# Query and key tiles in descending order in the attention and mLSTM tasks of a two-block transformer kernel

## The chip, the cores and the metric

The kernel runs on one core of one Trainium2 chip. The metric is device time in microseconds for one execution; lower is better.

## What is computed

Two transformer blocks follow one another on a sequence of 512 tokens with 1024 features, all in float32. The first has a mixer with two kinds of attention and a mixture of experts; the second has a mixer of native sparse attention and an mLSTM, a cross attention on a memory, and a feed-forward layer. The change touches only these parts (cut from the reference):

```python
# block 1, forget attention: 8 heads of 64; F is the running sum of log gates
s = jnp.einsum('bhqd,bhkd->bhqk', qb, k) * scale + Fq[..., :, None] - F[..., None, :]
p = jax.nn.softmax(jnp.where(pos[None, :] <= tq[:, None], s, -jnp.inf), axis=-1)
o = jnp.einsum('bhqk,bhkd->bhqd', p, v)
# block 1, differential attention: 4 heads, two maps of 64, values of 128
p1 = jax.nn.softmax(jnp.where(mask, s1, -jnp.inf), axis=-1)
p2 = jax.nn.softmax(jnp.where(mask, s2, -jnp.inf), axis=-1)
o = jnp.einsum('bhqk,bhkd->bhqd', p1 - lam * p2, v)
# block 2, sparse attention: 8 heads of 64 in 2 groups, three branches
return gc[..., 0:1] * o_c + gc[..., 1:2] * o_s + gc[..., 2:3] * o_w
# block 2, mLSTM: 4 heads, queries and keys of 64, values of 128
s = jnp.einsum('bthd,bshd->bhts', qc, kc) * w
num = jnp.einsum('bhts,bshv->bhtv', s, vc) + ...
```

All maps are causal (or causal by chunks), so query tile i of 128 rows needs key tiles 0 to i only.

## The kernel before

Everything is tiled by 128. A sequence is four query tiles (NT = 4). The program is written for a framework that inserts the semaphores and lets a compiler put the instructions of each engine in an order by a model of their times; the order of the program is their priority, not their final order. Projections are float32 products in three matmuls (`mm3`, lines 149 to 154: high by high, high by low, low by high).

**Tasks.** Attention is cut into tasks, each with a map of four query tiles: 8 Fox tasks (class `Fox`, line 444, one per head), 4 Diff tasks (class `Diff`, line 468), 16 NSA tasks (class `Nsa`, line 1420, two per head: b = 0 for the selected and b = 1 for the window branch), and 4 mLSTM cells (class `Cell`, line 1754). A task has these methods:

- `a(i)`: the scores of query tile i against key tiles 0 to i, 128*(i+1) wide, on TensorE into one of two "sc" banks (lines 440, 1468); `softmax_rows` (line 229) adds the bias and takes the row minimum on VectorE (line 237), then the exponential on ScalarE (line 239), into a tile "sx". Fox scales the row at once (lines 454, 455). Diff combines two maps into one row (lines 479 to 483). NSA scales rows in pairs after every second step (lines 1474 to 1483: factors L1476 and L1477, rows by VectorE at L1483, but row 2 by ScalarE at L1481).
- The transposes of the task: `transposer32` (line 260) makes key tile j of the transposed map in one of two "tr" banks: 4-j transposes, from rows j to 3 (line 269), then one copy (line 270) by ScalarE for even j and by VectorE for odd j.
- `finish`: the product of the transposed map with the values. Fox and NSA do it for two heads at a time, 16 matmuls of 64 columns (`apply_pair`, line 275, L280), so in every second Fox task and in the tasks of odd NSA heads; Diff (L495) and Cell (L1795) do it for each task. All begin with key tile 0.

**Order.** A task's rows are computed while the task before is transposed. Step i of four, in ascending order, is `cur.a(i)`, some fill, `trs(i)` of the task before, some fill; after the fourth step comes `prev.finish`. For Fox and Diff this loop is in `mixer1` (lines 526 to 546), for NSA and the cells in `run_tasks` (line 1219).

**Fill.** Projections wait in a queue in units of one k tile (three matmuls, `queue_proj`, line 117); `fill(n)` emits n of them. Fox emits one unit after every `a` and every `trs`; Diff one or two, in the last Diff task nearly none; NSA 1.25 a step after `a` and none after `trs`; the cells one after each.

**Beside the tasks.** In NSA, the short convolution of the mLSTM inputs runs in single steps (`conv`, line 1401: ScalarE L1410, GpSimd L1411, L1414, L1415); two steps are taken per task, after `a(0)` and `a(1)`, from the second head on. The lower halves of split weights go to GpSimd there (`share(0, 1)`, line 1534; L219), to VectorE elsewhere. In b = 1 tasks the next head's compressed branch is begun after `a(1)` (`compressed`, line 1431) and transposed after `a(3)` (`compressed_T`, line 1455, L1459).

**Buffers.** Rows are tiles "sx" of 128 x 512: 9 in mixer1 (SX) and 8 in the second block (SN). Diff's second map, the values before their transposition (`vt`, line 1392), the convolution temporary (`ct`, line 1409) and the cells' output (`yt`, line 1808) take tiles of the same rotation.

Of the kernel before, what the change touches and what calls it, by code (L numbers as in the profile page):

```python
# [30 lines left out]
SX = 9  # L31
SN = 8

# [61 lines left out]
class Builder:  # L95
# [132 lines left out]

    def softmax_rows(self, ps_s, i, win, pool, bufs, rs=None):

        nc = self.nc
        n = P * (i + 1)
        s = pool.tile([P, S], F32, tag="sx", name="sx", bufs=bufs)
        mn = pool.tile([P, 1], F32, tag="mn", name="mn", bufs=8)
        if rs is None:
            rs = pool.tile([P, 1], F32, tag="rs", name="rs", bufs=16)
        nc.vector.tensor_tensor_reduce(out=s[:, :n], in0=ps_s[:, :n], in1=win[:, S - P - P * i:S], scale=1.0,  # L237
                                       scalar=3.0e38, op0=ALU.add, op1=ALU.min, accum_out=mn)
        nc.scalar.activation(s[:, :n], s[:, :n], AF.Exp, bias=mn, scale=-1.0, accum_out=rs)  # L239
        return s, rs  # L240
# [97 lines left out]
    def mixer1(self, x_dram, outer, before_gates, before_out):  # L338
        nc, tc, a = self.nc, self.tc, self.a
        w_in = a["w_in"][0]  # L340
        with ExitStack() as st:
# [26 lines left out]
            with ExitStack() as sa:  # L368
# [75 lines left out]
                class Fox:  # L444
                    def __init__(s, h, box):
                        s.h, s.r, s.box, s.rows = h, h % 2, box, []

# [3 lines left out]
                    def a(s, i):  # L451
# [3 lines left out]
                        nc.vector.tensor_scalar_mul(p[:, :P * (i + 1)], p[:, :P * (i + 1)], rs)  # L455
                        s.rows.append(p)

# [10 lines left out]
                class Diff:  # L468
                    def __init__(s, h, box):
                        s.h, s.box, s.rows = h, box, []  # L470

# [3 lines left out]
                    def a(s, i):  # L475
                        n = P * (i + 1)
                        p1, r1 = self.softmax_rows(scores(s.box, 0, i), i, win[:, 1 + s.h], wk, SX)
                        p2, r2 = self.softmax_rows(scores(s.box, 1, i), i, win[:, 1 + s.h], wk, SX)
                        nc.vector.reciprocal(r2, r2)
# [3 lines left out]
                        nc.vector.scalar_tensor_tensor(p1[:, :n], p2[:, :n], r2, p1[:, :n], op0=ALU.mult, op1=ALU.add)  # L483
                        s.rows.append(p1)

# [29 lines left out]
                for g in range(8):  # L515
# [10 lines left out]
                    for r in range(2 if g < 4 else 1):  # L526
                        cur = Fox(2 * g + r, boxes[g]) if g < 4 else Diff(g - 4, boxes[g])
                        cur.start()
                        if prev is not None:
                            trs = self.transposer32(prev.rows, wk, pst, 3)  # L530
                        for i in range(NT):
                            cur.a(i)
                            self.fill(per[2 * i])
                            if prev is not None:
                                trs(i)
                            self.fill(per[2 * i + 1])
                        if prev is not None:
# [4 lines left out]
                trs = self.transposer32(prev.rows, wk, pst, 3)  # L542
                for j in range(NT):
                    trs(j)
# [674 lines left out]
    def run_tasks(self, tasks, slots, more, wk, pst, before, bufs):  # L1219

        prev, self.credit = None, 0
        for n, cur in enumerate(tasks + [None]):
# [3 lines left out]
            trs = self.transposer32(prev.rows, wk, pst, bufs) if prev is not None else None  # L1226
            for i in range(NT):
                if cur is not None:
# [65 lines left out]
    def mixer2(self, hT, sl, right):  # L1294
# [8 lines left out]
        with ExitStack() as sa:  # L1303
# [84 lines left out]
            def queue_v(h):  # L1388
                w = self.cols(w_in, 1816 + h * P)

                def done(z):
                    vt = wk.tile([P, S], F32, tag="sx", name="vt", bufs=SN)
                    nc.scalar.copy(vt, z)
# [7 lines left out]
            def conv(m):  # L1401
# [5 lines left out]
                for d in (3, 2, 1):  # L1407
                    c = 4 * (3 - d) + m
                    ct = wk.tile([P, S], F32, tag="sx", name="ct", bufs=SN)
                    nc.scalar.activation(ct[:, d:], u[:, :S - d], AF.Copy, scale=cw[:, c:c + 1])  # L1410
# [9 lines left out]
            class Nsa:  # L1420


                def __init__(s, h, b, head):
                    s.h, s.b, s.g, s.head, s.rows = h, b, h // 4, head, []

# [37 lines left out]
                def a(s, i):  # L1463
# [6 lines left out]
                    p, _ = self.softmax_rows(z, i, s.head["tab"], wk, SN, s.rs[:, i:i + 1])  # L1470
                    s.rows.append(p)
                    if i in (0,1) and s.h:
                        next(convs, None)
                    if i % 2 == 1:
                        c = slice(i - 1, i + 1)
                        nc.vector.reciprocal(s.rs[:, c], s.rs[:, c])  # L1476
                        nc.vector.tensor_mul(s.rs[:, c], s.rs[:, c], gates[:, c, 3 * s.h + 1 + s.b])  # L1477
                        for m in (i - 1, i):
                            n = P * (m + 1)
# [4 lines left out]
                    if s.b == 1 and s.h < 7:  # L1484
                        if i == 1:
                            self.drain(boxes[(s.h + 1) // 2])
                            tasks[2 * s.h + 2].compressed()
                        elif i == 3:
                            tasks[2 * s.h + 2].compressed_T()
# [234 lines left out]
    def mlstm(self, w_in, hT, mq, mv, mg, sl, right, work):  # L1724
# [29 lines left out]
        class Cell:  # L1754
            def __init__(s, h):
                s.h, s.rows = h, []

# [5 lines left out]
            def a(s, i):  # L1763
# [11 lines left out]
                                               op0=ALU.mult, op1=ALU.add, accum_out=s.den[:, i:i + 1])  # L1775
                s.rows.append(w)
                if i == 1 and s.h > 1:
                    cells[s.h - 2].after()
# [23 lines left out]
            def after(s):  # L1802
                h, on = s.h, s.on
                pt = pst.tile([P, S], F32, tag="tr", name="tr")
                for i in range(NT):
                    nc.vector.tensor_scalar_mul(on[:, i], on[:, i], s.r[:, i:i + 1])
                    nc.tensor.transpose(pt[:, i * P:(i + 1) * P], on[:, i], self.ident)
                yt = wk.tile([P, S], F32, tag="sx", name="yt", bufs=SN)
                nc.vector.scalar_tensor_tensor(yt, sg[:, h], 1.0, pt, op0=ALU.add, op1=ALU.mult)
# [177 lines left out]
```

## Time and profile before

| | |
|---|---|
| time, median of 3 runs | 1842.98 us (1830.79 to 1845.54) |
| profiled execution | 1842.04 us |
| its span, first to last instruction | 1840.3 us |
| granted TensorE clock, mean of the span | 0.981 |
| TensorE (PE) matmul busy | 1754.1 us, 95% |
| VectorE (DVE) / ScalarE (ACT) / GpSimd (POOL) busy | 834.3 / 590.9 / 101.5 us |

Times come from one profiled execution. PE is the matmul part of TensorE, PEld its weight load. A name such as `sx<-sx,nrs` gives the tile written and the tiles read; L1483 is line 1483 of the kernel. The granted clock is a share of full speed: 1.00 is 2.4 GHz, 0.50 is 1.2 GHz.

### The profile page before, as it was taken

The page shows a single profiled execution, that of the slowest core. Times are in us where ns is not written, and L with a number is a line of the kernel's source. Part 1 is how long each engine was busy: PE and PEld are TensorE (multiplying, and loading weights), DVE is VectorE, ACT ScalarE, POOL GpSimd, SP SyncE. Part 2 cuts the span into 40 slices and gives each one's busy share as a digit, 9 for nine tenths or more (in the row PEclk, how much of TensorE's full clock was granted, in tenths as well). Part 3 has the DMA queues.
Part 4 walks back from the last instruction along what each step waited for, and adds up shares of the span by engine and source line. Part 5 has one row for each costly group of instructions (what it writes and reads, how often), then busy time and mean ns, then how long its engine had stood idle before and what let it go on. Part 6 is the DMA issues. An engine that isn't in the chain of part 4 may idle for free. (4 is left out here: it accounts for less than half of the span.)

```text
span 1840.3 us, 21813 instructions
## 1 busy us (share of the span) xinstructions
PE 1754.1 (95%) x8295; PEld 1226.6 (67%) x8295; DVE 834.3 (45%) x2070; ACT 590.9 (32%) x1110; POOL 101.5 (6%) x100
## 2 busy tenths in 40 slices
PE   7899989999999999999999998999999999999998
PEld 5677767887655343333346876657797788888886
DVE  5488864336312221212107667667675643333224
ACT  4376732223100000000005557654444332232211
POOL 0000000011000000000001035200000000000000
PEclk9999999999999999999999999999999999999999
DMA  6221254347799999999977441102242233333221
GB/s 210 82 61 55 58 196 150 95 166 263 288 411 415 416 416 416 416 417 415 416 311 260 131 115 40 53 29 92 63 144 80 79 94 92 103 92 103 92 92 46
DMA packets 188985, 343.76 MB, mean 187 GB/s; under 512 B 14324, under 2 KB 136661, under 8 KB 172110
## 3 DMA queue, kind: packets, MB, share of 16 engines
q1 hardware_dynamic: 174768, 309.49, 46.1%
q0 software_dynamic: 8080, 25.07, 3.9%
q10 hardware_dynamic: 6030, 7.78, 1.2%
q8 instruction: 66, 1.08, 0.2%
q14 instruction: 41, 0.34, 0.1%
HBM read 330.74 MB, written 18.37 MB: 190 GB/s over the span
## 5 line engine op out<-in xcount | busy, mean ns | idle before, releaser
L219 DVE TENSOR_TENSOR wl<-wr,wh 128x1024 fp32r<-128x1024 f32 (+1 forms) x167 | 202.2, 1212 | 291.3 <-ACT wh L138 288.9
L138 ACT ACTIVATE wh<-wr 128x1024 fp32r<-128x1024 f32 (+1 forms) x178 | 186.0, 1050 | 446.3 <-PE mm L153 194.1
L152 PE MATMUL mm<-hTh,wh 128*128 128x512 f32 (+1 forms) x832 | 327.9, 395 | 0.7 <-ACT wh L138 0.7
L153 PE MATMUL mm<-hTl,wh 128*128 128x512 f32 (+1 forms) x832 | 320.2, 385 | 0.0
L154 PE MATMUL mm<-hTh,wl 128*128 128x512 f32 (+1 forms) x832 | 318.7, 383 | 0.6 <-DVE wl L219 0.6
L820 PE MATMUL mm<-we,xs 128*64 128x512 f32 x1024 | 241.4, 594 | 0.0
L154 PEld LDWEIGHTS mm<-hTh,wl 128*128 128x128 f32 x832 | 158.1, 190 | 31.0 <-DVE wl L219 1.1
L152 PEld LDWEIGHTS mm<-hTh,wh 128*128 128x128 f32 x832 | 158.2, 190 | 30.2 <-issue 3.3
L820 PEld LDWEIGHTS mm<-we,xs 128*64 128x64 f32 x1024 | 89.9, 137 | 129.3 <-issue 124.7
L153 PEld LDWEIGHTS mm<-hTl,wh 128*128 128x128 f32 x832 | 158.2, 190 | 23.4
L872 PE MATMUL sc<-we,hT 128*64 128x512 f32 x512 | 140.7, 599 | 1.7 <-issue 1.7
L872 PEld LDWEIGHTS sc<-we,hT 128*64 128x64 f32 x512 | 45.2, 136 | 75.5 <-issue 69.4
L858 DVE SCALAR_TENSOR_TENSOR h<-mm,rsl,h 128x512 f32<-128x512 f32 x16 | 12.0, 750 | 178.8 <-PE mm L820 178.8
L239 ACT ACTIVATE sx<-sx,mn 128x384 f32<-128x384 f32 (+3 forms) x128 | 71.4, 559 | 36.2 <-DVE mn L237 32.4
L875 ACT COPY yt<-sc 128x512 f32<-128x512 f32 x16 | 9.4, 586 | 194.5 <-PE sc L872 194.5
L786 DVE TENSOR_TENSOR xg<-tr,gmoe 128x512 f32<-128x512 f32 x32 | 22.1, 690 | 97.8 <-PE tr L784 97.8
L269 PE MATMUL tr<-ident,sx 128*128 128x128 f32 x320 | 60.5, 282 | 5.0 <-ACT sx L1481 2.5
L269 PEld LDWEIGHTS tr<-ident,sx 128*128 128x128 f32 x320 | 41.7, 144 | 23.2 <-ACT sx L1481 3.2
L784 PE MATMUL tr<-x1h,oh 128*128 128x512 f32 x128 | 53.9, 421 | 0.3 <-DVE xs L808 0.3
L784 PE MATMUL tr<-x1l,oh 128*128 128x512 f32 x128 | 51.7, 404 | 0.0
L808 ACT COPY xs<-tr 128x512 f32<-128x512 f32 x16 | 9.4, 587 | 130.5 <-PE tr L796 130.4
L876 DVE COPY yt<-sc 128x512 f32<-128x512 f32 x16 | 11.1, 691 | 76.8 <-PE sc L872 76.8
(597 smaller groups left out, 2938.7 us busy)
## 6 DMA issues: line engine op xcount, KB each, us to landing
we<-in_w_dram SPq DMA_DIRECT2D x126, 1024.0 KB, 15.0
we<-in_w_dram SPq DMA_DIRECT2D x132, 512.0 KB, 14.2
wr<-in_w_in_dram SPq DMA_DIRECT2D x60, 512.0 KB, 3.7
wr<-in_w_gate_up_dram SPq DMA_DIRECT2D x44, 512.0 KB, 3.7
wr<-in_w_down_dram SPq DMA_DIRECT2D x22, 512.0 KB, 3.4
wr<-in_w_o_dram SPq DMA_DIRECT2D x8, 512.0 KB, 3.2
wr<-in_w_xkv_dram POOLq DMA_DIRECT2D x8, 512.0 KB, 7.6
yc<-ybuf SPq DMA_DIRECT2D x8, 512.0 KB, 8.1
```

Of the source, the lines that this page charges most:

```text
L138: self.nc.scalar.activation(out, src, AF.Copy if isinstance(scale, float) else AF.Identity, scale=scale)
L152: mm(out, lhsT=lhs[0], rhs=rhs[0], start=start, stop=False)
L153: mm(out, lhsT=lhs[0], rhs=rhs[1], start=False, stop=False)
L154: mm(out, lhsT=lhs[1], rhs=rhs[0], start=False, stop=stop)
L219: next(self.lo_engines).tensor_sub(lo, raw, hi.bitcast(F32))
L239: nc.scalar.activation(s[:, :n], s[:, :n], AF.Exp, bias=mn, scale=-1.0, accum_out=rs)
L269: nc.tensor.transpose(pt[:, (i - j) * P:(i - j + 1) * P], rows[i][:, j * P:(j + 1) * P], self.ident)
L784: nc.tensor.matmul(pt, lhsT=oh[:, t], rhs=self.x1[m][:, t, c], start=t + m == 0, stop=t == NT - 1 and m == 1)
L786: nc.vector.tensor_mul(xg[:, c], pt, self.gmoe[:, c])
L820: self.nc.tensor.matmul(z[rr], lhsT=xs[:, k, rr], rhs=we[4 * m + 2 * (k // 4) + r][k % 4], start=k == 0, stop=k == KC - 1)
L858: nc.vector.scalar_tensor_tensor(h, us[1], rs, h, op0=ALU.mult, op1=ALU.mult)
L872: nc.tensor.matmul(zs[hf][rr], lhsT=hT[:, k, rr], rhs=we[8 + 2 * (k // 2) + r][k % 2][:, hf * 512:hf * 512 + 512], start=k == 0, stop=k == 3)
```

## The change

The four tasks' rows are computed for query tiles 3, 2, 1, 0, and the task before is transposed for key tiles 3, 2, 1, 0. Rows are kept in a dictionary by number. What hung on a step's number is moved to the step of the same place: the convolution steps to i = 3 and 2, `compressed` to i = 2, `compressed_T` to i = 0, the cells' `after` to i = 2. NSA scales rows 3 and 2 after the second step and rows 1 and 0 after the fourth. `finish` is unchanged and still begins with key tile 0. Diff's second map gets a tag "sy" with 2 buffers; `vt`, `ct` and `yt` get a tag "cv" with 2; SN goes from 8 to 9. The widths of the instructions and their number stay as they are.

```diff
-SN = 8
+SN = 9
...
-    def softmax_rows(self, ps_s, i, win, pool, bufs, rs=None):
+    def softmax_rows(self, ps_s, i, win, pool, bufs, rs=None, tag="sx"):
...
-        s = pool.tile([P, S], F32, tag="sx", name="sx", bufs=bufs)
+        s = pool.tile([P, S], F32, tag=tag, name=tag, bufs=bufs)
...
                         p1, r1 = self.softmax_rows(scores(s.box, 0, i), i, win[:, 1 + s.h], wk, SX)
-                        p2, r2 = self.softmax_rows(scores(s.box, 1, i), i, win[:, 1 + s.h], wk, SX)
+                        p2, r2 = self.softmax_rows(scores(s.box, 1, i), i, win[:, 1 + s.h], wk, 2, tag="sy")
...
-                        for i in range(NT):
+                        for n in range(NT):
+                            i = NT - 1 - n
                             cur.a(i)
-                            self.fill(per[2 * i])
+                            self.fill(per[2 * n])
                             if prev is not None:
                                 trs(i)
-                            self.fill(per[2 * i + 1])
+                            self.fill(per[2 * n + 1])
...
                 trs = self.transposer32(prev.rows, wk, pst, 3)
-                for j in range(NT):
+                for j in reversed(range(NT)):
                     trs(j)
                     self.fill(1)
...
             trs = self.transposer32(prev.rows, wk, pst, bufs) if prev is not None else None
-            for i in range(NT):
+            for i in reversed(range(NT)):
                 if cur is not None:
                     cur.a(i)
...
-                    vt = wk.tile([P, S], F32, tag="sx", name="vt", bufs=SN)
+                    vt = wk.tile([P, S], F32, tag="cv", name="vt", bufs=2)
...
-                    ct = wk.tile([P, S], F32, tag="sx", name="ct", bufs=SN)
+                    ct = wk.tile([P, S], F32, tag="cv", name="ct", bufs=2)
...
-                    s.rows.append(p)
-                    if i in (0,1) and s.h:
+                    s.rows[i] = p
+                    if i > 1 and s.h:
                         next(convs, None)
-                    if i % 2 == 1:
-                        c = slice(i - 1, i + 1)
+                    if i % 2 == 0:
+                        c = slice(i, i + 2)
...
-                        for m in (i - 1, i):
+                        for m in (i + 1, i):
...
-                        if i == 1:
+                        if i == 2:
                             self.drain(boxes[(s.h + 1) // 2])
                             tasks[2 * s.h + 2].compressed()
-                        elif i == 3:
+                        elif i == 0:
                             tasks[2 * s.h + 2].compressed_T()
...
-                if i == 1 and s.h > 1:
+                if i == 2 and s.h > 1:
                     cells[s.h - 2].after()
...
-                yt = wk.tile([P, S], F32, tag="sx", name="yt", bufs=SN)
+                yt = wk.tile([P, S], F32, tag="cv", name="yt", bufs=2)
```

## Rows read from the trace of the kernel before

**Rows 1.** The page, busy time of each engine, share of the span and instructions

```profile
PE 1754.1 (95%) x8295; PEld 1226.6 (67%) x8295; DVE 834.3 (45%) x2070; ACT 590.9 (32%) x1110; POOL 101.5 (6%) x100
```

**Rows 2.** Windows: length, busy time by engine, clock, DMA; Fox, Diff, NSA, mLSTM

```profile
85.00:165.00 80.00, 79.32 (x408) 59.92 (x406) 64.84 (x180) 57.68 (x128) 0.00 (x0) 1.00 0.22 60
165.00:250.00 85.00, 81.66 (x430) 62.99 (x429) 71.03 (x266) 53.69 (x141) 0.00 (x0) 1.00 0.26 75
1083.00:1226.00 143.00, 132.14 (x724) 93.60 (x724) 100.10 (x343) 96.95 (x240) 46.17 (x29) 0.96 0.15 45
1226.00:1290.00 64.00, 64.00 (x298) 44.93 (x297) 43.52 (x157) 28.41 (x72) 2.75 (x5) 0.89 0.23 79
```

**Rows 3.** Waits of TensorE (us, times, longest): Fox, then Diff, then NSA

```profile
PE tr L269 <- DVE sx L455: 0.7, 2, 0.5
...
PE mm L495 <- DVE on L497: 2.3, 2, 1.6
...
PE sc L1468 <- DVE mn L237: 3.6, 3, 2.5
PE tr L1459 <- DVE ce L1452: 2.9, 3, 1.6
PE tr L269 <- ACT sx L1481: 2.5, 2, 1.5
PE tr L269 <- DVE pT L270: 1.6, 1, 1.6
```

**Rows 4.** Windows with a reduced TensorE clock, in NSA and mLSTM

```profile
1144.00:1148.00 4.00, 4.00 (x14) 2.90 (x14) 3.93 (x15) 2.49 (x5) 2.87 (x3) 0.57 0.00 0
...
1172.00:1178.00 6.00, 5.35 (x19) 4.16 (x20) 3.76 (x14) 3.70 (x11) 0.00 (x0) 0.50 0.38 132
...
1233.00:1247.00 14.00, 14.00 (x33) 7.86 (x32) 5.39 (x17) 3.61 (x8) 0.00 (x0) 0.51 0.10 37
```

**Rows 5.** Timeline at a task's start in NSA: VectorE, then TensorE

```profile
1100.34 1.55 DVE L1477 TENSOR_TENSOR nrs<-nrs,gates 128x2 f32<-128x2 f32 x1
...
1100.77 0.39 PE L153 MATMUL mm<-hTl,wh 128*128 128x512 f32 x1
1102.64 0.44 PE L269 MATMUL tr<-ident,sx 128*128 128x128 f32 x2 [1.48 <-ACT sx L1481]
1102.84 0.48 PE L154 MATMUL mm<-hTh,wl 128*128 128x512 f32 x1
```

**Rows 6.** Timeline of TensorE in NSA: scores, then two units of fill

```profile
1157.87 0.71 PE L1468 MATMUL sc<-kk,qs 128*128 128x512 f32 x2
1158.41 0.40 PE L152 MATMUL mm<-hTh,wh 128*128 128x512 f32 x1
...
1159.11 0.40 PE L152 MATMUL mm<-hTh,wh 128*128 128x512 f32 x1
```

**Rows 7.** Groups of ScalarE in NSA (count, busy us, mean ns, idle before)

```profile
L1481 ACT ACTIVATE sx<-sx,nrs 128x384 f32<-128x384 f32 x16 | 9.8, 615 | 8.0 <-DVE nrs L1477 7.9
...
L270 ACT COPY pT<-tr 128x512 f32<-128x512 f32 x16 | 9.4, 585 | 7.1 <-PE tr L269 7.0
...
L270 ACT COPY pT<-tr 128x256 f32<-128x256 f32 x16 | 5.8, 366 | 2.5 <-PE tr L269 2.4
```

**Rows 8.** Timeline in NSA: VectorE, GpSimd and TensorE

```profile
1167.58 3.44 DVE L1483 TENSOR_SCALAR sx<-sx,nrs 128x128 f32<-128x128 f32 x2
...
1168.52 2.35 POOL L219 TENSOR_TENSOR wl<-wr,wh 128x1024 fp32r<-128x1024 f32 x1
...
1171.74 0.47 PE L1468 MATMUL sc<-kk,qs 128*128 128x128 f32 x1 [2.52 <-DVE mn L237]
```

**Rows 9.** Groups of VectorE: NSA's scaling, then Fox's scaling and copy

```profile
L1483 DVE TENSOR_SCALAR sx<-sx,nrs 128x128 f32<-128x128 f32 x16 | 9.8, 614 | 0.3
...
L455 DVE TENSOR_SCALAR sx<-sx,rs 128x128 f32<-128x128 f32 x8 | 2.3, 283 | 0.1
...
L270 DVE COPY pT<-tr 128x128 f32<-128x128 f32 x7 | 2.0, 286 | 0.1
```

More of the change, by code (lines that the diff above doesn't have):

```diff
@@ L445, in __init__ @@
                     def __init__(s, h, box):
-                        s.h, s.r, s.box, s.rows = h, h % 2, box, []
+                        s.h, s.r, s.box, s.rows = h, h % 2, box, {}
                     def start(s):
@@ L469, in __init__ @@
                     def __init__(s, h, box):
-                        s.h, s.box, s.rows = h, box, []
+                        s.h, s.box, s.rows = h, box, {}
                     def start(s):
@@ L483, in a @@
                         nc.vector.scalar_tensor_tensor(p1[:, :n], p2[:, :n], r2, p1[:, :n], op0=ALU.mult, op1=ALU.add)
-                        s.rows.append(p1)
+                        s.rows[i] = p1
                     def finish(s, aT):
@@ L1423, in __init__ @@
                 def __init__(s, h, b, head):
-                    s.h, s.b, s.g, s.head, s.rows = h, b, h // 4, head, []
+                    s.h, s.b, s.g, s.head, s.rows = h, b, h // 4, head, {}
                 def start(s):
@@ L1470, in a @@
                     p, _ = self.softmax_rows(z, i, s.head["tab"], wk, SN, s.rs[:, i:i + 1])
-                    s.rows.append(p)
-                    if i in (0,1) and s.h:
+                    s.rows[i] = p
+                    if i > 1 and s.h:
                         next(convs, None)
-                    if i % 2 == 1:
-                        c = slice(i - 1, i + 1)
+                    if i % 2 == 0:
+                        c = slice(i, i + 2)
                         nc.vector.reciprocal(s.rs[:, c], s.rs[:, c])
                         nc.vector.tensor_mul(s.rs[:, c], s.rs[:, c], gates[:, c, 3 * s.h + 1 + s.b])
-                        for m in (i - 1, i):
+                        for m in (i + 1, i):
                             n = P * (m + 1)
@@ L1755, in __init__ @@
             def __init__(s, h):
-                s.h, s.rows = h, []
+                s.h, s.rows = h, {}
             def start(s):
@@ L1775, in a @@
                                                op0=ALU.mult, op1=ALU.add, accum_out=s.den[:, i:i + 1])
-                s.rows.append(w)
-                if i == 1 and s.h > 1:
+                s.rows[i] = w
+                if i == 2 and s.h > 1:
                     cells[s.h - 2].after()
```

## The prediction

> **What bounds the kernel now.** I read the page first: TensorE is busy for 95% of a span of 1840.3 us [rows 1], so only what keeps TensorE waiting, or makes it slow, can move the time; work of the other engines is free as long as it stays beside TensorE. Next I cut the span by stage [rows 2]. The change touches four stretches: the Fox tasks (85 to 165 us), the Diff tasks (165 to 250), the NSA tasks (1083 to 1226) and the mLSTM cells (1226 to 1290), 372 us together. TensorE lacks 80 - 79.3 = 0.7 us in Fox, 85 - 81.7 = 3.3 in Diff, 143 - 132.1 = 10.9 in NSA and nothing in mLSTM. Idle time is thus 15 us in all, 0.8% of the span. A second loss hides in the clock: granted clock 0.96 in NSA and 0.89 in mLSTM. Then I asked who holds TensorE in each stretch [rows 3]. In Fox the whole 0.7 us is transposes waiting for a scaled row; in Diff 2.3 us are matmuls of `finish` waiting for evictions; in NSA 3.6 us are scores behind the row minimum on VectorE, 2.9 the compressed branch's transposes, 2.5 transposes behind a row scaled on ScalarE, and 1.6 transposes behind the eviction of an earlier one. Last I looked at where the clock falls [rows 4]: three stretches at or near the lower level of 1.2 GHz, two of them right behind a wait (1144 and 1172 us), the longest (1233 to 1247) behind the thin end of NSA.
>
> **The change part by part.** The sum is made against the profiled execution, 1842.0 us (span 1840.3 plus 1.7 outside it), 1 us under the median of 1843.0; the three runs lie 15 us apart, so about 1%, 18.4 us, is what a measurement of this kernel can tell from no change.
>
> *The transposes at a task's start.* Before, the first transposes of a task read column tile 0 of all four rows, and row 3, the widest, is the last that the task before has computed. The trace shows the price [rows 5]: the factors of rows 2 and 3 (L1477, two numbers a partition) are ready only at 1101.9, row 2 is scaled on ScalarE after that, and the transposes stand 1.48 us. Descending, a task's first transpose needs only row 3, computed three steps earlier, and row 0 is needed last. The dependency gains three steps of slack. I take all of these waits away: 2.5 + 0.7 = 3.2 us. The ends: nothing, if the held VectorE queue stops the next score instead, and 3.2. The same rows show that TensorE's order is not the program's: transposes stand inside a projection unit (L153, then L269, then L154). The compiler has already moved ready work into the gaps that it foresaw; that is why Fox has so little left.
>
> *The eviction wait, 1.6 us.* There are two transpose banks, so a task's fourth group waits for the second's eviction: before a VectorE copy, beside the scaling of step two; after, a ScalarE copy. It may equally recur at the third group. I take half, -0.8 (ends 0 and -1.6).
>
> *The clock.* The 4 us from 1144 run at 0.57; at the full 2.4 GHz they would take 2.3, so 1.7 us come back if the wait before them (1.0 of the 2.5) is gone. I count 1.7. The 6 us from 1172 (3.0 us lost) follow another wait, and the 14 us from 1233 (6.9 lost) a stretch without a wait to remove; they stay. Ends: 0 and -11.6.
>
> *The end of a task.* Before, the last group is one 128-wide transpose, copied by VectorE in 0.29 us [rows 9], and `finish` begins with tile 0, long evicted. After, the last group is tile 0 itself, four transposes and a 512-wide ScalarE copy of 0.585 us [rows 7], and `finish` reads it first. With an estimated 0.4 us for the transposes to end (0.44 us for two) [rows 5] and the hand-over, that is 1.0 us. Cover: in Fox, Diff and mLSTM one projection unit stands between, 0.70 us from the first L152 to the next [rows 6]; in NSA none does, but the next task's 512-wide scores (0.54 by the same rows) or, with the window branch not yet open, the two matmuls on the compressed values are ready. Uncovered: 0.3 x 12 + 0.5 x 4 = 5.6 us over 20 finishes if the order stayed the program's. As the compiler moves ready work in, I take a third, +1.9. Ends: 0 and 20 x 1.0 = 20; without any cover it is the upper end.
>
> *The compressed branch.* `compressed` still follows the second step of every second task and `compressed_T` the fourth, in 7 tasks. Between them lie the scores of two rows: 384 and 512 wide before, 256 and 128 after, which takes less cover away than the 0.54 us of one 512-wide pair [rows 6]. And ScalarE's queue in front of the branch's exponential grows: the copy of 256 (0.37) and the scaling of row 2 (0.62) now lie in step two, up to 1.0 us [rows 7]. VectorE has narrower rows behind it in return. Ends: -2.9 (the present waits vanish) and 7 x (1.0 + 0.54) = 10.8; three of seven show a wait now, so I stay near zero, +1.0.
>
> *Convolution steps* stay in the first two steps of a task, so GpSimd's work falls where it fell. *Buffers:* no instruction is added. Rows are now held to the end of the next task, 4 old and 4 new out of 9; the ninth serves the first row of the following task, and the second waits for transposes that stand before its own scores on TensorE: nothing. `sy` and `cv` get two buffers each; a second map is used up within its step and a convolution temporary by the next GpSimd instruction: nothing. The ends for the three together: -1 and +1.
>
> Sum: -3.2 - 0.8 - 1.7 + 1.9 + 1.0 = -2.8 us, 1842.0 - 2.8 = 1839 us.
>
> **A rule against the change.** The dearest NSA wait stands in the timeline [rows 8]: two scalings (L1483, 128 and 256 wide) last 3.44 us, up to the end of a GpSimd instruction, and the scores behind them stand 2.52 us. None of this depends on which row is scaled. By the Trainium skill, "SBUF — State Buffer", section "Who interferes with whom", VectorE and GpSimd share a port pair as an exclusive lock, and whichever issues second is blocked for the whole instruction. The trace agrees: the 128-wide scaling takes 614 ns in the mean in NSA and 283 in Fox, where GpSimd has no work [rows 2, 9]. By that rule the new second step, whose scaling is 512 wide, is blocked just as long, and the 3.6 us of waits behind the minimum stay; by the descending order alone one might have hoped to lose them too and written 1839 - 3.6 = 1835.
>
> **The rivals.**
> *All waits go (faster).* If three steps of slack let TensorE's queue never dry up in NSA, its 10.6 us of named waits, Diff's 2.3 and Fox's 0.7 go, 13.6 in all, and with them the clock stretches (11.6): 1842 - 25 = 1817. For it: the clock falls behind waits. Against: only 3.2 us of the waits hang on row order, and the stretch at 1233 has none before it. It decides if at least 18 of the 25 go. The middle case, in which the long stretch stays, gives 1842 - 13.6 - 4.7 = 1824.
> *Every finish waits (slower).* The mechanism is the last part but one above: tile 0 comes last and `finish` reads it first. If the compiler finds nothing to put between, 20 finishes cost 1.0 us each, and with the other terms as above (-4.7) that is 1842 - 4.7 + 20 = 1857; with one more ScalarE instruction of 0.6 us [rows 7] in front of each copy, 1869. It is over 1% from (18.4 + 4.7) / 20 = 1.2 us per finish. For it: NSA has no unit in between and ScalarE is busy for 97 of 143 us [rows 2]. Against: 12 of the 20 have 0.70 us of cover, and the order is the compiler's.
> *It does nothing.* The waits were the compiler's misjudgement of GpSimd, not of row order, and show up at another instruction: 1842.
>
> **How the numbers follow.** Forecast 0.55, range of its own 1833 to 1846; nothing 0.20; all or nearly all waits go 0.14, of which 0.09 lie beyond 1%; every finish waits 0.11, of which 0.09 beyond 1%. So faster by over 1% 0.09, within 1% 0.82, slower 0.09. The range takes in the middle case on the fast side, 1824, less 1, and on the slow side the finish wait at two thirds of its price: 1842 - 4.7 + 13 = 1850, and 1 more.
>
> **What would show it right or wrong.** Right: in the waits of the new trace TensorE's L269 no longer waits for a scaled row (L455, L1481); a task begins with one transpose and ends with four, then a 512-wide ScalarE copy; L280 and L495 wait now and then for that copy, under 0.5 us each; the wait for the minimum stays near 3.6 us. Wrong on the fast side: NSA shorter than 135 us, granted clock 1.00 throughout. Wrong on the slow side: L280, L495 or L1795 with 10 us or more of idle time behind L270, or the compressed transposes behind ScalarE.

## The result, and the profile after

The changed kernel takes 1857.83 us (median of 10 runs, 1853.72 to 1867.53) against 1842.72 us for the kernel before (10 runs, 1830.79 to 1848.38): a ratio of 1.0092, 95% interval 1.0073 to 1.0110. It is 15 us slower; 1839 was predicted, with a range up to 1851. In this kernel one line was added, so lines behind line 531 have a number higher by one (L1468 is L1469 now).

The profiled execution (1855.07 us, span 1853.3, granted clock 0.979) looks no worse by its summary. First the engines as in [rows 1], then the windows as in [rows 2], moved to where the stages lie now:

```profile
PE 1763.7 (95%) x8295; PEld 1235.2 (67%) x8295; DVE 831.4 (45%) x2070; ACT 591.8 (32%) x1110; POOL 101.0 (5%) x100
```

```profile
85.00:165.00 80.00, 79.05 (x408) 60.87 (x406) 63.96 (x180) 59.09 (x128) 0.00 (x0) 1.00 0.23 60
165.00:252.00 87.00, 83.55 (x431) 64.25 (x432) 70.61 (x265) 52.89 (x140) 0.00 (x0) 1.00 0.25 72
1090.00:1238.00 148.00, 138.26 (x737) 99.29 (x738) 99.16 (x346) 94.32 (x235) 40.07 (x24) 0.97 0.16 44
1238.00:1306.00 68.00, 65.77 (x303) 45.93 (x302) 44.69 (x163) 27.73 (x70) 3.27 (x6) 0.90 0.24 81
```

TensorE is busy for 9.6 us more with the same 8295 matmuls. That is the line to stop at: part of the loss does not appear as idle time. From the first NSA score on, idle time even fell, from 10.9 to 9.7 us (most of the wait of 3.8 us shown next lies ahead of this window), but the stretch is longer. TensorE's waits there and in the cells, as in [rows 3]:

```profile
PE sc L1439 <- DVE mn L237: 4.2, 2, 2.3
PE sc L1439 <- DVE qs L1381: 3.8, 1, 3.8
PE tr L1460 <- ACT mq L1414: 2.1, 1, 2.1
PE tr L1460 <- DVE ce L1453: 1.9, 1, 1.9
PE sc L152 <- DVE den L1775: 1.8, 1, 1.8
PE mm L280 <- ACT pT L270: 0.4, 1, 0.4
...
PE tr L269 <- DVE pT L270: 0.2, 1, 0.2
```

No transpose waits for a scaled row any more. Two waits are new: 3.8 us for the first query split (`qs`) and 1.8 us in the cells. And the scores that stand behind the row minimum are now those of the compressed branch (L1439), no longer those of the two other branches. In Diff, 2.2 us of L495 now stand behind the copy L270, in place of the 2.3 behind L497.

To place the 13.0 us between the two profiled spans, I compared the start of the same instruction in both traces. Each row shows how late the changed kernel is there:

| TensorE instruction (number of before) | before, us | later by |
|---|---|---|
| first Fox score, L440 | 91.7 | 0.4 |
| first matmul behind the first mixer, L607 | 267.3 | 1.8 |
| last L1645, ahead of the last unit of projections | 1068.1 | 4.1 |
| first NSA score, L1438 | 1083.0 | 7.6 |
| first L1760, start of the cells | 1229.7 | 9.1 |
| last L1760, start of the last cell | 1270.3 | 9.1 |
| first L1876, cross attention | 1373.8 | 11.9 |
| end of the span | 1840.3 | 13.0 |

So 1.4 us are lost in the first mixer, 3.5 at the start of NSA, 1.5 net within NSA, and 2.8 behind the start of the last cell, of which 1.7 are a clock stretch of 3.4 us at 1288; most of the rest is where the clock fell between stages (6.8 us at the lower level at 435 us, against 3.4, and 3.4 us at 1476, against none).

**The time that hides in busy TensorE.** The products of `finish` in NSA handle two heads, each in its own 64 columns. Two runs of 16 such products from TensorE's timeline, the kernel before and then the changed one:

```profile
1121.76 2.37 PE L280 MATMUL mm<-pT,vs 128*64 128x512 f32 x16
```

```profile
1172.44 3.27 PE L280 MATMUL mm<-pT,vs 128*64 128x512 f32 x16
```

The same 16 products take 0.9 us more, with no gap between them. (The trace records each float32 product twice, so these are 8 products of four key tiles and two heads.) By the trace's start times the first run issues both heads' first products 7 ns apart and the next pair 480 ns after the first. In the second run the newer head's first product starts 903 ns behind the other head's, because its weight load (PEld, here the second line) waits for the copy of key tile 0; from then on the heads run out of step.

```profile
1172.44 0.19 PEld L280 LDWEIGHTS mm<-pT,vs 128*64 128x64 f32 x2 [0.17 <-issue]
1173.34 0.20 PEld L280 LDWEIGHTS mm<-pT,vs 128*64 128x64 f32 x4 [0.71 <-ACT pT L270]
```

In the kernel before, three of the eight runs of 16 are in step from end to end; in the changed kernel, none is. The groups show the loss as well (NSA, TensorE by shape; xcount, busy us, mean ns): before, then after:

```profile
L280 PE MATMUL mm<-pT,vs 128*64 128x512 f32 x32 | 12.9, 618 | 0.0
L280 PE MATMUL mm<-pT,vs 128*64 128x384 f32 x32 | 10.2, 496 | 0.0
...
L280 PE MATMUL mm<-pT,vs 128*64 128x128 f32 x32 | 5.2, 280 | 0.0
```

```profile
L280 PE MATMUL mm<-pT,vs 128*64 128x512 f32 x32 | 16.7, 618 | 0.4 <-ACT pT L270 0.4
L280 PE MATMUL mm<-pT,vs 128*64 128x384 f32 x32 | 13.2, 497 | 0.0
...
L280 PE MATMUL mm<-pT,vs 128*64 128x128 f32 x32 | 6.1, 273 | 0.0
```

A single product lasts as long as before (618 ns). What grew is the union of their times: 32 products of 618 ns would be 19.8 us one after the other, and 12.9 us of union means that most ran in pairs. By the Trainium skill, "TensorEngine Tiling (Array Packing)", section "Key Properties", different tiles of the array can load weights and multiply in parallel; the trace agrees, with starts 7 ns apart and with 2.37 against 3.27 us for the same work.

Since busy time includes overlap with neighbours, I use a stricter count below: each L280 and L1500 from its start to the next start on TensorE, without idle time; a product that starts at the lower clock level is counted half. In NSA that is 29.9 us before and 33.2 after: +3.3 us.

### The profile page after: what moved, and what is told of

It reads as the page before. It is cut to its first block, busy times and chain, and to the rows that moved or that the text cites. A ratio compares the mean times of both kernels' runs of the same rounds, so it can differ in the third digit from the quotient of the medians.

```text
span 1853.3 us, 21811 instructions
## 1 busy us (share of the span) xinstructions
PE 1763.7 (95%) x8295; PEld 1235.2 (67%) x8295; DVE 831.4 (45%) x2070; ACT 591.8 (32%) x1110; POOL 101.0 (5%) x100
## 5 line engine op out<-in xcount | busy, mean ns | idle before, releaser
L239 ACT ACTIVATE sx<-sx,mn 128x512 f32<-128x512 f32 (+1 forms) x112 | 62.5, 558 | 31.4 <-DVE mn L237 30.1
L269 PE MATMUL tr<-ident,sx 128*128 128x128 f32 x320 | 58.3, 280 | 0.6 <-DVE pT L270 0.2
L269 PEld LDWEIGHTS tr<-ident,sx 128*128 128x128 f32 x320 | 41.2, 144 | 15.1 <-DVE pT L270 1.6
```

The costliest lines, as they stand in the source:

```text
L269: nc.tensor.transpose(pt[:, (i - j) * P:(i - j + 1) * P], rows[i][:, j * P:(j + 1) * P], self.ident)
```

## The experiments

All ratios are to runs of the kernel before on the same chip, with 95% intervals; no kernel leaves out any part of the computation. "Products" is the strict count for NSA; "low clock" is the time at 1.2 GHz from the last L1645 (1068 us in the kernel before) to the end of the cells, in the profiled execution.

The last column uses every execution, not the profiled one alone. Each has its span and its mean granted clock on record: span times clock estimates how long it would take at 2.4 GHz throughout ("at full clock"), and the rest of the span is what the lower level took ("lost"). Both are means, less those of the kernel before on the same chip (for the changed kernel's first line, of its 97 executions on all chips). The kernel before, measured once more, shows the noise: about 1 us at full clock and 2 us in the loss.

| kernel | ratio | products, us | low clock, us | at full clock / lost, us |
|---|---|---|---|---|
| before, as shown / once more (e11) | 1.0000 (0.9984 to 1.0016) | 29.9 / 29.8 | 23.9 / 27.3 | e11: -0.8 / +0.3 |
| changed | 1.0092 (1.0073 to 1.0110) | 33.2 | 23.9 | +9.0 / +7.8 |
| changed, once more (e10) | 1.0081 (1.0061 to 1.0101) | 33.0 | 51.2 | +9.0 / +6.9 |
| e1 changed, `ct` among the rows | 1.0058 (1.0044 to 1.0071) | 31.9 | 13.7 | +7.0 / +2.5 |
| e3 changed, cells ascending | 1.0041 (1.0027 to 1.0056) | 32.9 | 17.1 | +8.1 / +0.1 |
| e4 changed, first mixer ascending | 1.0060 (1.0043 to 1.0076) | 32.9 | 30.7 | +6.8 / +4.8 |
| e5 changed, products descending | 1.0021 (1.0004 to 1.0038) | 29.6 | 10.2 | +6.1 / -1.9 |
| e6 changed, convolution behind first query | 1.0075 (1.0052 to 1.0098) | 33.3 | 17.1 | +6.5 / +6.8 |
| e8 changed, e3 + e5 + e6 | 1.0015 (0.9999 to 1.0031) | 30.3 | 13.7 | +2.1 / +0.7 |
| e12 only NSA descending, with its products | 0.9990 (0.9974 to 1.0006) | 29.6 | 10.2 | +2.1 / -3.9 |
| e2 before, `ct` in own buffers | 0.9972 (0.9958 to 0.9985) | 29.7 | 6.8 | +0.7 / -5.8 |
| e7 before, e2 + convolution behind first query | 0.9960 (0.9941 to 0.9978) | 29.6 | 6.8 | -1.0 / -6.4 |
| e9 before, products descending | 0.9954 (0.9938 to 0.9970) | 27.2 | 10.2 | -3.1 / -5.5 |
| e13 before, e7 + e9 | 0.9955 (0.9939 to 0.9970) | 28.2 | 10.2 | -0.1 / -7.7 |
| e14 before, e2 + e9 | 0.9982 (0.9964 to 0.9999) | 28.2 | 10.2 | -0.5 / -3.7 |

### Products that read the last tile last: e5 and e9

The same edit, put on the changed kernel (e5) and on the kernel before (e9):

```diff
-        for j in range(NT):
+        for j in (range(NT) if last else reversed(range(NT))):
...
-                                      stop=stop and j == NT - 1)
+                                      stop=stop and j == last)
...
-                    self.apply_pair(o, [lambda j: vs[:, j, 2 * s.b + s.g]] * 2, [t.pT for t in heads], False, s.b == 1)
+                    self.apply_pair(o, [lambda j: vs[:, j, 2 * s.b + s.g]] * 2, [t.pT for t in heads], False, s.b == 1, 0)
```

Expected of e5: 

> The changed kernel, with one edit: in the NSA tasks the products of finish (L281) take the key tiles in descending order too, so that the tile evicted last is read last. Theory F (the products of two heads fill the two halves of TensorE's columns side by side only while both streams are ready; after the change the newer head's first product waits for the last eviction, and the halves run one after the other, as in 3.27 us for 16 products against 2.37): L281 and L1502 together, counted from start to next start without idle time, fall from 33.2 us to 30 or less in the NSA stretch; time 1857.8 - 3.3 = 1854.5 us. Theory A (only the start of NSA matters) and theory B (only the cells): 1858 within 2 us, and the 33 us stay.

Expected of e9: 

> The kernel before (rows and transposes ascending, buffers as before), with one edit: the NSA products of finish read the key tiles in descending order, so that here the tile evicted last, 128 columns wide, is read first. Theory F (the price of a finish that reads the last tile first is the time in which only one half of TensorE's columns has work, so it grows with the width of that tile): the break now falls on the 128-wide products and not on the 512-wide ones; L280 and L1500 together fall from 29.9 us to 28 to 29.5, the time is 1842.7 - 1 = 1842 us, within 2, no loss. If reading the last tile first costs a wait whatever its width (the rival as the prediction had it, 1 us per finish of NSA): 1842.7 + 8 = 1851 us.

e5 took 1844.79 us: one edit removes 13 of the 15 us. (The profile has the two product lines of the text above as L280 and L1501.) The run of 16 is back at its old length, though it starts with the tile that was 128 wide:

```profile
1168.78 2.39 PE L280 MATMUL mm<-pT,vs 128*64 128x128 f32 x16
```

The products fall from 33.2 to 29.6 us, as theory F asked, but that is 3.6 us, not 13. Of the 12.1 us between the two profiled spans, 6.8 more are the clock: 10.2 us at the lower level in this part instead of 23.9; half of the difference is lost time. Another 1.4 us lie ahead of the first Fox score, which the edit doesn't touch. Over all executions the edit gives 2.9 us at full clock and 9.7 of clock loss. So the direct cost of the products is shown, and so is that the clock loss falls with this edit. That products out of step bring on the clock stretches is not shown: e3 leaves the products out of step and loses 7.7 us less to the clock as well.

e9 settles what sets the price. In it, too, the tile evicted last is read first, but it is 128 wide. The rival, a wait of 1 us per finish whatever the width, said 1851; F said 1842 within 2. It took 1834.17: the products fell to 27.2 us, below what F gave, and the stretch at 1233 [rows 4] went. None of the eight runs of 16 is in step here, yet by the strict count they take 2.58 to 2.70 us, against 3.04 to 3.37 in the changed kernel, 3.09 to 3.59 for the five of the kernel before that were out of step already, and 2.30 in step: a lone product costs by its width. The rival falls; F keeps its mechanism and missed the size, of the time above all, since 5.5 us of the gain are clock and 3.1 are not.

### Buffers of its own for the convolution: e1, e2, e6, e7

e1 puts `ct` back among the rows (12 of them so that none waits, and one buffer for `vt`); e2 makes only that part of the change on the kernel before:

```diff
# e1, on the changed kernel
-                    ct = wk.tile([P, S], F32, tag="cv", name="ct", bufs=2)
+                    ct = wk.tile([P, S], F32, tag="sx", name="ct", bufs=12)
# e2, on the kernel before
-                    ct = wk.tile([P, S], F32, tag="sx", name="ct", bufs=SN)
+                    ct = wk.tile([P, S], F32, tag="cv", name="ct", bufs=2)
```

Expected of e1: 

> The changed kernel, but the convolution's temporary ct takes its buffer from the rotation of the rows again (12 of them, so that no row waits); order of the rows as changed. Theory A (the buffer of its own let the compiler place two convolution channels ahead of the first query split on ScalarE; TensorE then waits 3.8 us at 1090.6 and runs 6.8 us at the lower clock level): that wait is gone, the first query split follows L1407 directly, the NSA scores start at least 5 us earlier against the last expert matmul, and the time is 1857.8 - 7 = 1851 us. Theory B (the descending order costs most, in the mLSTM tail): the first score is earlier or not, but the lateness comes back before the end: 1855 to 1858. Theory L (it is the phase of the clock's falls that the edits merely shift): no relation, any value from 1845 to 1862, with the granted-clock stretches elsewhere.

Expected of e2: 

> The kernel before, rows ascending everywhere, with one edit: ct has two buffers of its own. Theory A: the convolution runs ahead of the first query split on ScalarE, TensorE waits for that split by some 4 us at the start of the NSA tasks and its clock falls there; 1842.7 + 7 = 1850 us. Theory B (only the order costs): within 2 us of 1843. Theory L: within 4 us of 1843 on either side.

The reason for theory A stood in ScalarE's and TensorE's timelines of the changed kernel, at the start of NSA:

```profile
1079.60 0.80 ACT L1407 ACTIVATE cy<-mq,vec 128x512 f32<-128x512 f32 x1
1080.31 1.32 ACT L1411 ACTIVATE ct<-mq,vec 128x509 f32<-128x509 f32 x2
1082.41 0.72 ACT L1411 ACTIVATE ct<-mq,vec 128x511 f32<-128x511 f32 x1 [0.78 <-POOL cy L1412]
1083.78 0.72 ACT L1411 ACTIVATE ct<-mq,vec 128x509 f32<-128x509 f32 x1 [0.65 <-POOL cy L1412]
1085.15 0.63 ACT L1414 ACTIVATE mq<-cy 128x512 f32<-128x512 f32 x1 [0.65 <-POOL cy L1412]
1085.69 0.71 ACT L1411 ACTIVATE ct<-mq,vec 128x510 f32<-128x510 f32 x1
1088.52 0.81 ACT L1407 ACTIVATE cy<-mq,vec 128x512 f32<-128x512 f32 x1 [2.12 <-POOL mq L1416]
1089.24 0.57 ACT L1380 ACTIVATE qs<-mm 64x512 fp32r<-64x512 f32 x1
```

```profile
1090.58 1.68 PE L1439 MATMUL sc<-kcp,qs 128*128 128x32 f32 x7 [3.77 <-DVE qs L1381]
```

e1 took 1850.55 us, A's number. ScalarE has its old order at the start of NSA again, and TensorE does not wait there. The first NSA score is 0.9 us behind the kernel before instead of 7.6, but most of that was won ahead of the last L1645, where the edit changes nothing; from there to the first score it takes 16.6 us, after 18.4 in the changed kernel and 14.9 before, and 1.7 of it are a clock stretch at 1075. Its low clock is 13.7 us against 23.9, and one buffer for `vt` brings a wait of 1.4 us of its own (L1397), so the time alone does not prove A: at full clock the edit gives 2.0 us, not 7.

With no row in its way, a convolution channel and more was put ahead of the first query split, and each step waits for GpSimd in ScalarE's queue. In the kernel before that split ran at 1081.66 and TensorE did not wait. e2, where no order was changed, has the same 3.8 us wait, and its first NSA score loses 3.4 us from the last L1645 on; so the buffer does this, not the order. But e2 is faster than the kernel before (0.9972), where A said 1850: NSA from its first score to its last takes 4.7 us less, 1.7 of them clock, and the stretch at 1233 is gone. At full clock the early convolution thus costs at the start what it saves in the tasks (+0.7 us over all executions); what e2 gains is clock. A named a real wait and was wrong about its worth.

e6 and e7 keep the buffers and hold the convolution back by its bias, which passes through a small tile written from the first query split, times zero:

```diff
-            cw, cb = self.gcol("conv_w_2"), self.gcol("conv_b_2")
+            cw, cb = self.gcol("conv_w_2"), wk.tile([P, 4], F32, name="cbq", bufs=1)
...
             self.drain()
+            nc.vector.scalar_tensor_tensor(cb, boxes[0][1][:, 0:4].bitcast(F32), 0.0, self.gcol("conv_b_2"),
+                                           op0=ALU.mult, op1=ALU.add)
```

Expected of e6: 

> The changed kernel, with one edit: the convolution's bias goes through a small tile that is written from the first query split (times zero, plus the bias), so that no convolution channel can be completed ahead of that split; buffers and order as changed. Theory A (ScalarE's queue at the start of NSA): the 3.8 us wait behind L1381 goes, the first NSA score comes 3.5 us earlier, the clock stretch of 6.8 us there goes or moves, 1857.8 - 5 = 1853 us. Rival A2 (the early convolution also takes GpSimd and ScalarE work out of the NSA tasks, so what is won at their start is lost in them): the first score is earlier, but the last NSA score is not; 1857 us within 2.

Expected of e7: 

> The kernel before (rows ascending everywhere), with ct in two buffers of its own and the bias tile of the run above. Theory A: the gain of the buffers without their price at the start of NSA: 1836.5 - 5 = 1831.5 us. Rival A2: the early convolution is where the gain of the buffers came from, so it goes back to the kernel before: 1840 to 1843 us.

In e6 the 3.8 us wait is gone and the first score comes right after the projections. From the first NSA score to the last L1469, though, it takes 3.9 us more than the changed kernel, so the win is given back, and 1855.41 us is within rival A2 and not clear of the changed kernel's time. But 3.4 of the 3.9 are clock (17.1 us at the lower level in that stretch, after 10.2), so the time fits A2 without its mechanism: at full clock e6 keeps 2.5 us. In e7 most of it was kept: 1832.76 us, close to A's 1831.5; of its 4.0 us at the start the NSA tasks took back 1.7. By their intervals, e7 (0.9941 to 0.9978) and e2 (0.9958 to 0.9985) are not to be told apart.

### Cells and first mixer ascending: e3, e4

```diff
# e3
-        self.run_tasks(cells, 1, 1, wk, pst, before, 2)
+        self.run_tasks(cells, 1, 1, wk, pst, before, 2, True)
# e4
-                            i = NT - 1 - n
+                            i = n
```

(In e3 the loop of `run_tasks` ascends with that flag, and the cells' `after` is back at i = 1; in e4 the last loop of transposes ascends too.)

Expected of e3: 

> The changed kernel, but the mLSTM cells take their rows in ascending order again (buffers as changed). Theory B (the tail of the cells costs 4.6 us: after the last 128-wide row nothing is left for TensorE while VectorE finishes the denominators, and the clock falls): the stretch from the last L1761 to the last out-projection transpose falls from 26.4 to about 22 us, the 1.8 us wait behind L1776 is gone; 1857.8 - 4.6 = 1853 us. Theory A alone: unchanged, 1858 within 2 us.

Expected of e4: 

> The changed kernel, but the Fox and Diff tasks of the first mixer take their rows in ascending order again. Theory C (in Diff, finish reads the last evicted tile first: 2.2 us of L495 behind the ScalarE copy): that wait goes back to under 0.5 us behind the copy of tile 0, the memory branch's first matmul is 1 to 2 us earlier; 1857.8 - 2 = 1856 us. Theories A and B: 1858 within 2 us.

e3 took 1850.60 us, and the wait of 1.8 us (behind L1775 in the profile) is gone. VectorE's timeline in the changed kernel, then in e3, shows why it was there:

```profile
1285.93 1.23 DVE L219 TENSOR_TENSOR wl<-wr,wh 128x1024 fp32r<-128x1024 f32 x1 [0.57 <-ACT wh L138]
...
1287.15 0.42 DVE L1775 CUSTOM_DVE_ANT_0 sx<-sc,sx 128x256 f32<-128x256 f32 x1
...
1287.78 0.87 DVE L1807 TENSOR_SCALAR on<-on,lrz 128x128 f32<-128x128 f32 x4
```

```profile
1284.72 0.88 DVE L1807 TENSOR_SCALAR on<-on,lrz 128x128 f32<-128x128 f32 x4
1285.78 1.23 DVE L219 TENSOR_TENSOR wl<-wr,wh 128x1024 fp32r<-128x1024 f32 x1 [0.18 <-ACT wh L138]
```

Descending, the last cell's scores end on the 128-wide row. The score banks that the next projections need come free only when VectorE reaches L1775, behind a weight split of 1.23 us, and the transposes of L1807's output, which could have filled the gap, come later still. Ascending, these stand ahead of the split. The stretch from the last L1761 to the last L1808 falls from 26.3 to 21.7 us, as expected. In e5, e6 and e10, which keep the order of the cells and have no clock stretch there, it is 24.7; so 3.0 us are the order's and 1.6 the clock stretch at 1288. By the cross attention 2.8 us of the 4.6 are still there in the changed kernel, 1.1 without the clock. That is the direct price, and it agrees with the 0.9 us at full clock that e3 gains over all executions. The rest of e3's 7 us is clock: 17.1 us at the lower level against 23.9, and 7.7 us less loss over all executions.

In e4 the first mixer gets its 1.4 us back (the products of Fox are 9.2 us again by the strict count, after 10.1, and L440 22.5 after 23.5; no L495 waits for the copy any more), close to theory C's 1 to 2. Its time, 1853.26 us, fell by some 3 us more than that; over all executions it gains 2.2 us at full clock and 3.0 of clock loss.

### Together: e8, e12, e13, e14

Expected of e8: 

> The changed kernel with all three edits: cells ascending, NSA products descending, convolution behind the first query split. If theories A, B and F are separate and add up: 1857.8 - 5 - 4.5 - 3.3 = 1845 us, so that the descending order of the first mixer and of NSA is left with a cost of some 2 us over the kernel before. By A2 1849 us. If a part of the cost was only the phase of the clock: 1850 or more.

Expected of e12: 

> Descending order in the NSA tasks alone, with their products descending too and ct in its own buffers; first mixer and cells ascending. By the ledger of the runs so far: the run with products descending (1844.8) less 1.4 for the first mixer and 2.5 for the cells = 1841 us. If the descending order has a gain of its own in NSA once the products are in step (the boundary wait of 3.2 us that the prediction counted): below the 1836.5 us of the same kernel with NSA ascending. If it has none or the compressed branch takes it: 1840 or more.

Expected of e13: 

> The kernel before (rows ascending), with ct in two buffers of its own, the bias tile that keeps the convolution behind the first query split, and the NSA products in descending key order. If the gains are separate terms (-10.5 for the first two edits, -9 for the products): 1843 - 19 = 1824 us. If both gains hold the one clock stretch of 13.7 us at the start of the cells (6.8 us of time): 1843 - 19 + 7 = 1831 us.

Expected of e14: 

> As the run above without the bias tile. If separate: 1843 - 5 - 9 = 1829 us, and TensorE waits 3.8 us at the start of NSA; if the stretch is shared: 1835 us. Against the run above it is 4 us slower by theory A, equal by rival A2 (what the start of NSA loses, its tasks give back).

e8 (1844.03 us) is no better than e5 alone (1844.79), where adding up gave 1845 from a smaller gain for e5. At full clock it is 4.0 us better than e5; it loses 2.6 us more to the clock. e12 (1840.56) and e14 (1837.76) differ in the order of the NSA rows and, beside it, only in the number of row buffers and in the buffers of `vt`, `yt` and Diff's second map: 0.9990 and 0.9982, not to be told apart. So no time shows a gain of the descending order in NSA, even with products that suit it; at full clock it is 2.6 us behind. It does take away the waits for scaled rows, but the compressed branch stands longer (L1460 behind `ce`: 6.6 us in e12, L1459 2.4 in e14). e13 (1834.42) is as fast as e7 or e9 alone, not at 1824: the gains share what they remove, and what they share is clock, 5.5 to 7.7 us less loss in each of the three. e14, the same without the bias tile, has the wait of 3.8 us again and is 3.3 us slower, near theory A's 4; but the two are alike at full clock (-0.1 and -0.5), as rival A2 said, and differ by 4.0 us in what the clock takes. The fastest versions are thus the kernel before with one or two edits, e7, e9 and e13, all 0.4 to 0.5% under it and not to be told apart.

### Both kernels once more: e10, e11

Expected of e10: 

> The changed kernel once more, to see which of its stretches at the lower clock level belong to the program and which to the one execution. If the stretches at 1090 (6.8 us), 1247 (10.2) and 1288 (3.4) are the program's, they come back at the same places, and the median is 1858 within 2. If the one at 1247 is only phase, it is elsewhere or gone in this profile, and single times spread by 5 us or more.

Expected of e11: 

> The kernel before once more, for the same reason: the stretch of 13.7 us at 1233 comes back at the same place if it is the program's; else the profile's span is up to 7 us shorter. The waits for ce, mn, sx and pT in the NSA tasks are the same within 0.5 us, since they hang on the program's order.

The stretch at the start of the cells belongs to the program in the kernel before: it came back at the same place. These are windows of e11, of the changed kernel at its two stretches, of e10 and of e5:

```profile
1233.00:1247.00 14.00, 14.00 (x33) 8.19 (x33) 6.15 (x20) 3.77 (x9) 0.00 (x0) 0.52 0.12 39
```

```profile
1090.00:1098.00 8.00, 7.42 (x25) 6.53 (x26) 4.18 (x14) 4.52 (x11) 6.25 (x4) 0.57 0.25 68
1247.00:1258.00 11.00, 11.00 (x27) 6.52 (x26) 3.96 (x13) 3.30 (x7) 0.00 (x0) 0.53 0.11 45
```

```profile
1157.00:1175.00 18.00, 17.25 (x48) 10.09 (x50) 6.54 (x27) 8.77 (x20) 4.86 (x4) 0.53 0.17 44
1260.00:1274.00 14.00, 14.00 (x36) 8.80 (x36) 5.93 (x16) 3.48 (x7) 0.00 (x0) 0.51 0.13 38
```

```profile
1233.00:1247.00 14.00, 14.00 (x53) 7.91 (x51) 9.72 (x27) 4.96 (x11) 0.00 (x0) 1.00 0.11 39
```

In the changed kernel the stretch behind NSA comes back as well (at 1247 and, in e10's later time, at 1260), but inside NSA the clock varies from execution to execution: e10 has 18 us at 0.53 there, and its span was 1865.8 us with the same instructions. (This execution, at 1867.64 us, was the slowest of seven; their median is 1857.59.) Its waits in NSA and the cells are the same to 0.1 us, but for one more of 1.2 us (L1469 behind the minimum). In e11 the waits equal those of [rows 3] but for `ce`, 2.2 us after 2.9.

## Why the prediction was wrong

**Right: what the order removes.** The boundary waits (-3.2 us) went, and with them the eviction wait: over the whole kernel the idle time in front of L269 fell from 5.0 to 0.6 us, where the two terms together said -4.0. The waits behind the minimum stayed, 4.2 us after 3.6, as the rule on VectorE's and GpSimd's shared port (the Trainium skill, "SBUF — State Buffer", section "Who interferes with whom") had led to expect. But other instructions are concerned than the prediction named. The 512-wide scaling of the second step is never held (0.47 to 0.49 us in all 16 tasks). Both waits follow a factor instruction of two numbers a partition (L1478), which lasts 1.88 and 1.84 us, up to the end of a GpSimd weight split, where another of its kind takes 0.16; the compressed branch's scores stand behind it. Here GpSimd, VectorE and TensorE at the first of the two:

```profile
1110.01 2.40 POOL L219 TENSOR_TENSOR wl<-wr,wh 128x1024 fp32r<-128x1024 f32 x1 [11.52 <-ACT wh L138]
...
1110.55 1.88 DVE L1478 TENSOR_TENSOR nrs<-nrs,gates 128x2 f32<-128x2 f32 x1
...
1114.51 1.06 PE L1439 MATMUL sc<-kcp,qs 128*128 128x32 f32 x8 [1.87 <-DVE mn L237]
```

In every edited version with ascending rows (e2, e7, e9, e13, e14) the waits behind the minimum are 0.7 to 0.8, and e9 has the convolution where the kernel before has it; so neither the row order alone nor the convolution's place sets them. The compressed branch cost 4.0 us of waits after 2.9 (L1460), +1.1 where +1.0 was said.

**Wrong: "the end of a task", +1.9 us.** The place was right: tile 0 comes last and `finish` reads it first. The form was not. I priced a wait, asked which work would cover it, and took a third; for NSA the sum had four finishes, where there are eight. The compiler did find cover, and there is 0.4 us of idle time behind L270 in NSA. But the cover stands between, or beside, two products that had run in the two halves of TensorE's columns at once. The measured term is +3.3 us in NSA and +0.9 in Fox (9.2 to 10.1 us), 4.2 together, and in Diff the waits of `finish` only changed their releaser. Undoing it in NSA brought 13 us in all, 2.9 of them at full clock. The rival "every finish waits" gave 1857 with this mechanism and had 0.11; the time came out there, but its sign, 10 us or more of idle behind L270, did not, so the match is luck.

**Wrong: "Convolution steps stay in the first two steps of a task" and buffers "nothing".** I read the order of the program and had said myself that it is not the final order. In the old rotation a row's buffer had tied the convolution to the tasks; the buffer of its own untied it, and the compiler moved it to the start of NSA: 3.5 us there. Its end of +1 was too near. The same freedom gained 5 us on the kernel before (e2), but in the clock: at full clock it is +0.7.

**Not in the sum: the last cell.** I costed the cells' end only through `finish`. The new wait of 1.8 us and what follows it cost 2.8 us of the profiled span, 1.7 of them clock.

**Wrong: the clock, -1.7 us.** The stretch at 1144 stayed (3.4 us at 1145), behind another wait; in the two profiles the low clock of this part is 23.9 us each. But over all executions the changed kernel loses 7.8 us more to the clock than the kernel before (e10, profiled, has 51.2 us). No term missed by more: with the 9.0 us at full clock it makes 16.8 us between the means, 15 between the medians.

With the measured terms the sum for the profiled span is 1.4 (first mixer) + 3.5 (start of NSA) + 1.5 (NSA: products +3.3, less idle time in return) + 2.8 (last cell) = 9.2 of the 13.0 us.

**What stays open.** Undoing one of four parts (e1, e3, e4, e5) took 5 to 13 us off each, in sum more than twice the 15 us there were. At full clock they add up: 2.0, 0.9, 2.2 and 2.9 make 8.0 of the 9.0 us, and e3, e5 and e6 make 6.3 singly and 6.9 together (e8). So the direct part of the loss is accounted for, within the noise, and it is the clock's part that the runs share, above all the stretch at the start of the cells, which is there in both kernels, in two pieces of 6.8 us in e4, in part (3.4 us) in e3 and e13, and gone in the others. All runs with products of 32.9 us or more spent 17 us or more at the lower level, but so does the kernel before with 29.9. What decides whether that stretch comes was not found, so the cause of the clock's part stays open.

## What to carry to other kernels

Work that keeps an engine busy can still be lost: when two streams share TensorE by column halves, compare the union of their times with their number times their mean, and give them operands that become ready together, the narrowest late one first. A buffer of its own is a freed instruction: ask where a scheduler may now put it, and which queue it will block. When one wait is priced by its cover, ask also what the cover breaks apart. And where the clock varies between executions, split each time by its granted clock before calling a difference the price of an edit.

## What the runs showed of the hardware

Two products of 64 columns and 512 wide start 7 ns apart in the trace, and their two records take 480 and 430 ns to the next start (kernel before, at 1121.8 us); a product without a partner took 480 and 423 ns (changed kernel, at 1172.4 us): a lone half costs about as much as a pair. The same program, profiled twice, had 23.9 and 51.2 us of its NSA tasks and cells at the lower clock level.
